# The recurrent unit of an encoder block in another order: both directions gated and scanned first, far halves inverted before the keys, each near half inverted beside the states

## The chip, the cores and the metric

The kernel runs on one core of a Trainium2 chip. The metric is the device time of one execution, in microseconds (us). A core has five engines with an instruction queue each: TensorE (PE) for matrix products and transposes, VectorE (DVE), ScalarE (ACT) and GpSimd (POOL) for elementwise work, and SyncE (SP), which here only issues DMAs. An instruction waits at the head of its engine's queue until what it needs is there, and all behind it wait too.

## The reference

One layer of an encoder for a sequence of 1024 tokens of width 1024. A layer norm, one large projection, dilated window attention with 24 heads, a bidirectional gated recurrence (HGRN2) with 8 heads, a gated merge, and a SwiGLU feed-forward, each with its layer norm:

```python
h = layer_norm(x, ln_in_g, ln_in_b)
proj = h @ w_in[l]                     # 1024 x 11776
aq, ak, av, hq, hf_fwd, hf_bwd, hi, hg, ga, gh = jnp.split(proj, split_idx, axis=-1)
att = dilated_attention(aq, ak, av, slopes)
rec = hgrn2(hq, hf_fwd, hf_bwd, hi, hg, lower_bounds[:, l], hgrn_norm_g[l])
merged = jax.nn.sigmoid(ga) * (att @ w_att_up[l]) + jax.nn.sigmoid(gh) * (rec @ w_hgrn_up[l])
h = layer_norm(DEEPNORM_ALPHA * h + merged @ w_o[l], ln1_g[l], ln1_b[l])
```

The change touches `hgrn2` alone. Per head and direction, with gate f = lb + (1 − lb)·sigmoid(...), key k = 1 − f, query q = silu(...)·128^-0.5 and value v, the chunkwise form is:

```python
q_dec = q * jnp.exp(cum)               # cum: running sum of log f in a chunk
k_inv = k * jnp.exp(-cum)
a = jnp.where(causal_in_chunk, jnp.einsum('bhnik,bhnjk->bhnij', q_dec, k_inv), 0.0)
o_intra = jnp.einsum('bhnij,bhnjv->bhniv', a, v)
u = jnp.einsum('bhnck,bhncv->bhnkv', k * jnp.exp(cum_last - cum), v)
state = d[..., None] * state + uu      # carried from chunk to chunk
o_inter = jnp.einsum('bhnck,bhnkv->bhncv', q_dec, s_start)
```

## The kernel before

**Stages.** The projection (to about 1145 us), the merge with the output projection and a layer norm, and the two halves of the feed-forward. The change lies in the projection stage, `phase1`.

**The stream of products.** `stream` computes the projection by a Strassen-like scheme: a block of 1024 x 512 weights takes 14 products (seven, in the order 1, 2, 6, 5, 7, 3, 4, each for two groups g of columns), and 23 blocks make 322 products. A product is twelve matmuls of 128x128 by 128x512: four slices of k by three terms (L270 to L272), since each operand is split in a high part `hi` and a rest `lo`. ACT makes `w_hi` (L212), POOL `w_lo` (L222), three products ahead. The sums of weights which the scheme needs are made five products ahead: on DVE L652 (`ws`), L653 and L657 (`wa`), on POOL L654. Finished products leave PSUM by `leave`: ACT keeps a copy (`wkeep`, L680), DVE adds the copy to the next product (`plain` L531, `tanhs` L542, `silu2` L556 and L558, with ACT's tanh L557 between them), and a DMA on SP's queue stores the result. Each group has two PSUM banks (tiles `pj`), used in turn.

**The side units.** While the stream runs, one side unit at a time is advanced beside it: `phase1` counts products, and each `yield n` of a unit lets n products pass before its next step. There are eight units `hgrn_side` (one for each recurrent head, in four pairs, a pair after each two heads' columns) and the attention units. Their small products and transposes go to PSUM tiles `sd`.

**One recurrent head.** A chunk has 128 tokens. A direction d has a half of it that is near the place to which the decays are related (`R`, in the buffer `fb`, 8 x 66 columns) and a far half (`A`, one half of the buffer `fa`). `hgrn_dir` does for a direction: ACT makes the gates (L1103 and L1108 into `fa`, L1104 and L1109 into `fb`), POOL sets border columns (L1102, L1107) and makes the keys `t` (L1110); DVE scans `fa` and `fb` to running products (L1115); POOL multiplies the near keys by `R` (L1123). After a yield DVE takes reciprocals of the far half (L1126) and the near half (L1129), in two instructions each of 128 x 256 elements, into the tile `qd`; POOL multiplies the far keys (L1127); DVE multiplies the queries of the far half (L1130) and of the near half (L1131); POOL copies and multiplies three columns `dec` (L1135 to L1137). So the reciprocals of a direction stand right behind its scans, four in a row.

`hgrn_side` goes through direction 0, then 1, loads the output gate `hg` (L734, SP's queue; its buffer is the `fb` of direction 1), transposes the values (L743), and then takes the transposed keys of direction 0 (PE L1145, ACT's copy `hkT` L1146), its states (PE L1161; ACT writes `hS`, L1163, over `fa`; DVE L1169), the keys and states of direction 1, the scores (L1186 to L1190, POOL's sum `ham` L1195), the output (L1212), and the last transposes (L1248) with the gate (DVE L1250, `hg`). ACT's queue issues the store `rec<-hg` (L1251). The buffer of `hg` is the next head's `fb` of direction 1, so that head's L1107 and L1109 wait for this store.

**What sets the order.** The program is written with the Tile framework, whose scheduler places each engine's instructions by simulated readiness and priority. Evictions and weight sums have a priority 1000 steps ahead. `left` notes an eviction by DVE as the latest, and `behind` puts an instruction behind it in the engine's order; it is an order only and no wait. In the kernel before, `behind` is used for the weight sums (L652, L657).

Of the kernel before, what the change touches and what calls it, by code (L numbers as in the profile page):

```python
# [14 lines left out]
OP = mybir.AluOpType  # L15
# [19 lines left out]
CQ = 0.5 * 128 ** -0.5  # L35
# [44 lines left out]
class Block:  # L80
# [152 lines left out]
        self.issued[key] = ins.ins.name  # L233
        return ins

    gone = None

    def left(self, ins):
        self.gone = ins.ins.name

    def behind(self, ins, last=None):

# [848 lines left out]
    def hgrn_dir(self, h, d, st):  # L1091

        nc = self.nc
        ga, gb, gna = (z[:, d, h:h + 1] for z in (self.ga, self.gb, self.gna))
        t3 = st[f"t{d}"].rearrange("p (c i) -> p c i", i=128)
        q3 = st["q"].rearrange("p (c i) -> p c i", i=128)

        A = st["fa"][:, HALF * d:HALF * d + HALF].rearrange("p (c i) -> p c i", i=64)
        B = self.slot(7 + d, "fb", (8, 66))
        if d == 0:  # L1100
            nc.gpsimd.memset(A[:, :, 0:1], 0.0)
            nc.gpsimd.memset(B[:, :, 65:66], 0.0)  # L1102
            nc.scalar.activation(A[:, :, 1:64], t3[:, :, 65:128], AF.Identity, bias=gb, scale=ga)  # L1103
            nc.scalar.activation(B[:, :, 0:65], t3[:, :, 0:65], AF.Identity, bias=gb, scale=ga)  # L1104
        else:
            nc.gpsimd.memset(A[:, :, 63:64], 0.0)
            nc.gpsimd.memset(B[:, :, 0:1], 0.0)  # L1107
            nc.scalar.activation(A[:, :, 0:63], t3[:, :, 0:63], AF.Identity, bias=gb, scale=ga)  # L1108
            nc.scalar.activation(B[:, :, 1:66], t3[:, :, 63:128], AF.Identity, bias=gb, scale=ga)  # L1109
        nc.gpsimd.tensor_scalar(t3, t3, gna, ga, op0=OP.mult, op1=OP.add)  # L1110

        def scan(f, n, rev):
            f = f.rearrange("p c i -> p (c i)")
            f = f[:, ::-1] if rev else f
            nc.vector.tensor_tensor_scan(f, f, self.d1[n], 0.0, op0=OP.mult, op1=OP.add)  # L1115

        scan(A, 64, d == 1)
        scan(B, 66, d == 0)
        far = slice(64, 128) if d == 0 else slice(0, 64)
        near = slice(0, 64) if d == 0 else slice(64, 128)  # L1120
        R = B[:, :, 1:65]
        qd = self.slot(2 + 2 * d, "qd", (8, 128))
        nc.gpsimd.tensor_mul(t3[:, :, near], t3[:, :, near], R)  # L1123
        yield
        for c in (slice(0, 4), slice(4, 8)):
            nc.vector.reciprocal(qd[:, c, far], A[:, c])  # L1126
        nc.gpsimd.tensor_mul(t3[:, :, far], t3[:, :, far], qd[:, :, far])  # L1127
        for c in (slice(0, 4), slice(4, 8)):
            nc.vector.reciprocal(qd[:, c, near], R[:, c])  # L1129
        nc.vector.scalar_tensor_tensor(qd[:, :, far], q3[:, :, far], CQ, A, op0=OP.mult, op1=OP.mult)  # L1130
        nc.vector.scalar_tensor_tensor(qd[:, :, near], q3[:, :, near], CQ, qd[:, :, near], op0=OP.mult, op1=OP.mult)  # L1131
        st["qd", d], st["ki", d] = qd, t3

        dec = st["dec", d] = self.smt.tile([128, 3, 8], F32, name="dec", tag="dec", bufs=4)
        nc.gpsimd.tensor_copy(dec[:, 0, :], A[:, :, 63 if d == 0 else 0])  # L1135
        nc.gpsimd.tensor_copy(dec[:, 1, :], B[:, :, 0 if d == 0 else 65])
        nc.gpsimd.tensor_mul(dec[:, 2, :], dec[:, 0, :], dec[:, 1, :])  # L1137

    def hgrn_keys(self, st, d):

# [9 lines left out]
    def hgrn_states(self, st, d, kT, vT):  # L1150


        nc, dec = self.nc, st["dec", d]
        S = self.slot(6 + d, "hS", (8, 128))
        cs = list(range(8)) if d == 0 else list(range(7, -1, -1))
# [66 lines left out]
    def hgrn_side(self, h, st):  # L1222
        nc = self.nc
        v = self.fetch(5, "hv", self.hg_d[h]["v"])
        st["fa"] = self.slot(6, "fa")
        for d in range(2):
            for _ in self.hgrn_dir(h, d, st):
                yield 1
            if d == 0:
                yield 1  # L1230
        sg = self.fetch(8, "hg", self.hg_d[h]["g"])
        yield 1
        vT = self.turned(v.rearrange("p (k d) -> p k d", k=8), lambda c: v[:, 128 * c:128 * c + 128])
        k0 = self.hgrn_keys(st, 0)
        yield 3
        S = {0: self.hgrn_states(st, 0, k0, vT)}
        k1 = self.hgrn_keys(st, 1)
        yield 3
        S[1] = self.hgrn_states(st, 1, k1, vT)
        yield 3  # L1240
        am = [self.hgrn_scores(st, b) for b in range(2)]
        yield -2
        on = [self.hgrn_out(st, b, am[b], vT, S) for b in range(2)]
        yield 2
        for b in range(2):
            pt = self.ps_sd()
            for jj in range(4):
                nc.tensor.transpose(pt[:, 128 * jj:128 * jj + 128], on[b][:, jj, :], self.ident)  # L1248
            s = slice(HALF * b, HALF * (b + 1))
            nc.vector.scalar_tensor_tensor(sg[:, s], pt, self.ngc, sg[:, s], op0=OP.mult, op1=OP.mult)  # L1250
        nc.scalar.dma_start(self.rec_d[h], sg)  # L1251
# [661 lines left out]
```

## Time and profile before

| | |
|---|---|
| median of three runs | 2074.36 us (2071.59, 2074.36, 2077.41) |
| the profiled execution | 2071.3 us, its span 2069.5 us |
| granted TensorE clock in it | 0.994 |
| PE busy | 2016.2 us, 97% of the span |
| DVE busy | 1325.4 us, 64% |
| POOL busy | 1074.7 us, 52% |
| ACT busy | 953.8 us, 46% |

A row of a group reads: line, engine, operation, output <- inputs, count | busy us, mean ns of one | idle time of the engine just before, and what ended it. A row of a timeline reads: start in us from the beginning of the span, duration, engine, line, operation. A row of a list of waits reads: engine and line of the waiting instruction, what it waited for, and then total us, number of times and the longest. Matmuls are pipelined: each shows about 0.39 us, though they start closer together, so a group of them says less of the time than their starts do. A queue's own waits carry a q behind the engine's name (ACTq, SPq).

### The profile page before, as it was taken

How to read it: one execution, taken by the hardware profiler on the slowest of the kernel's cores; microseconds unless marked ns; L12 is line 12 of the kernel's file. 1: busy time of each engine (PE TensorE's matmuls, PEld its weight loads, DVE VectorE, ACT ScalarE, POOL GpSimd, SP SyncE). 2: the span in 40 equal slices, each digit the busy share in tenths (PEclk: the TensorE clock that was granted, in tenths of full speed). 3: DMA queues.
4: the chain of work that ended last, by engine and by line, in shares of the span. 5: the costliest groups of instructions: out<-in, count | busy, mean ns of one | idle time of the engine just before them, and what ended most of it. 6: DMA issues, size and time to landing. Idle time of an engine off the chain costs nothing. (4 is left out here: it accounts for less than half of the span.)

```text
span 2069.5 us, 30921 instructions
## 1 busy us (share of the span) xinstructions
PE 2016.2 (97%) x10974; PEld 1669.0 (81%) x10974; DVE 1325.4 (64%) x2017; ACT 953.8 (46%) x1968; POOL 1074.7 (52%) x919
## 2 busy tenths in 40 slices
PE   7899999999999999999999999999999999999998
PEld 5688888888887888888888888787888888888876
DVE  6966645884368744776343225547776776758777
ACT  6554455553655436454365432244433333334542
POOL 5766744776356653665536662344665665620012
PEclk9999999999999999999999999999999999999999
DMA  5443433435333452344524376444444443447423
GB/s 157 133 139 125 158 122 105 157 126 173 97 123 133 131 163 93 122 139 137 166 93 154 124 249 219 154 145 139 154 137 138 133 137 132 144 158 270 164 89 127
DMA packets 274844, 297.95 MB, mean 144 GB/s; under 512 B 14017, under 2 KB 207362, under 8 KB 274690
## 3 DMA queue, kind: packets, MB, share of 16 engines
q1 hardware_dynamic: 268384, 274.78, 41.0%
q10 hardware_dynamic: 6306, 21.20, 2.6%
q8 instruction: 86, 1.41, 0.3%
q14 instruction: 68, 0.56, 0.1%
HBM read 201.29 MB, written 94.63 MB: 143 GB/s over the span
## 5 line engine op out<-in xcount | busy, mean ns | idle before, releaser
L222 POOL TENSOR_TENSOR w_lo<-wa,w_hi 128x512 fp32r<-128x512 f32 x272 | 363.2, 1345 | 277.8 <-ACT w_hi L212 250.3
L212 ACT CAST w_hi<-wa 128x512 fp32r<-128x512 f32 x272 | 168.4, 620 | 251.0 <-PE pj L271 165.3
L222 POOL TENSOR_TENSOR w_lo<-wsum,w_hi 128x512 fp32r<-128x512 f32 x88 | 127.7, 1460 | 111.3 <-PE sd L272 60.7
L222 POOL TENSOR_TENSOR w_lo<-f_raw,w_hi 128x512 fp32r<-128x512 f32 x66 | 102.1, 1555 | 55.2 <-ACT w_hi L212 54.0
L208 POOL TENSOR_TENSOR mv<-mv,mhalf 128x1 f32<-128x1 f32 x16 | 10.8, 680 | 208.3 <-DVE mv L207 208.2
L212 ACT CAST w_hi<-wsum 128x512 fp32r<-128x512 f32 x88 | 54.7, 621 | 122.2 <-PE sd L271 118.7
L270 PE MATMUL pj<-xt1hi,w_hi 128*128 128x512 f32 x252 | 99.8, 396 | 3.6 <-DVE evh L531 1.9
L270 PE MATMUL pj<-xb22hi,w_hi 128*128 128x512 f32 x252 | 99.3, 394 | 0.0
L272 PE MATMUL pj<-xb22hi,w_lo 128*128 128x512 f32 x252 | 98.5, 392 | 0.4 <-POOL w_lo L222 0.3
L542 DVE TENSOR_TENSOR evh<-wkeep,pj 128x512 f32<-128x512 f32 x45 | 30.8, 684 | 106.4 <-PE pj L272 61.2
L271 PE MATMUL pj<-xb22lo,w_hi 128*128 128x512 f32 x252 | 98.5, 391 | 0.0
L272 PE MATMUL pj<-xt1hi,w_lo 128*128 128x512 f32 x252 | 98.5, 391 | 0.0
L271 PE MATMUL pj<-xt1lo,w_hi 128*128 128x512 f32 x252 | 98.3, 390 | 0.0
L212 ACT CAST gwsum<-a_raw 128x512 fp32r<-128x512 f32 (+1 forms) x78 | 47.7, 616 | 101.6 <-PE pj L271 47.2
L654 POOL TENSOR_TENSOR wa<-wa,wa 128x512 f32<-128x512 f32 x46 | 65.1, 1424 | 49.5 <-DVE wa L653 44.0
L680 ACT COPY wkeep<-pj 128x512 f32<-128x512 f32 x136 | 79.4, 584 | 21.6 <-DVE evh L558 11.9
L531 DVE TENSOR_TENSOR evh<-wkeep,pj 128x512 f32<-128x512 f32 x66 | 57.5, 879 | 44.5 <-PE pj L272 33.9
L222 POOL TENSOR_TENSOR w_lo<-ws,w_hi 128x512 fp32r<-128x512 f32 x46 | 63.2, 1378 | 43.1 <-ACT w_hi L212 42.9
L222 DVE TENSOR_TENSOR gwkeep<-a_raw,gwsum 128x512 fp32r<-128x512 f32 (+1 forms) x78 | 57.7, 739 | 42.0 <-ACT gwsum L212 39.1
L270 PE MATMUL pj<-xt4hi,w_hi 128*128 128x512 f32 x192 | 76.4, 398 | 3.5 <-DVE evh L531 2.4
L272 PE MATMUL pj<-xt2hi,w_lo 128*128 128x512 f32 x192 | 75.5, 394 | 3.7 <-POOL w_lo L222 3.7
L270 PE MATMUL pj<-xb11hi,w_hi 128*128 128x512 f32 x192 | 76.8, 402 | 1.3 <-DVE wkeep L556 1.3
(421 smaller groups left out, 6585.1 us busy)
## 6 DMA issues: line engine op xcount, KB each, us to landing
wa<-in_w_in_dram SPq DMA_DIRECT2D x184, 256.0 KB, 3.3
f_raw<-in_w_ffn_in_dram SPq DMA_DIRECT2D x44, 512.0 KB, 4.0
a_raw<-gd SPq DMA_DIRECT2D x30, 512.0 KB, 3.6
gd<-fc SPq DMA_DIRECT2D x44, 256.0 KB, 2.0
gd<-fs SPq DMA_DIRECT2D x33, 256.0 KB, 2.1
tg<-evh SPq DMA_DIRECT2D x32, 256.0 KB, 2.3
tg<-tg SPq DMA_DIRECT2D x16, 512.0 KB, 3.6
y<-ahs SPq DMA_DIRECT2D x16, 512.0 KB, 4.6
```

What stands on the lines that cost most here:

```text
L208: nc.gpsimd.tensor_tensor(mv[:, 2:3], mv[:, 2:3], self.mhalf[:, 0:1], OP.pow)
L212: ins = nc.scalar.copy(hi, src) if eng_hi == "act" else nc.vector.tensor_copy(hi, src)
L222: ins = e.tensor_sub(lo, src, hi.bitcast(F32))
L270: nc.tensor.matmul(ps, whi, xhi, start=first, stop=False, **kw)
L271: nc.tensor.matmul(ps, whi, xlo, start=False, stop=False, **kw)
L272: self.product = nc.tensor.matmul(ps, wlo, xhi, start=False, stop=last, **kw).ins.name
L531: self.left(nc.vector.tensor_tensor(o, self.order_src(add, g, kind), s, OP.add))
L542: self.left(nc.vector.tensor_add(t, add, ps))
L654: nc.gpsimd.tensor_sub(a["a21"], a["a22"], a["a11"])
L680: nc.scalar.copy(t, ps)
```

## The change

`hgrn_dir` becomes a sequence of five steps with a yield between them, and `hgrn_side` calls the steps of the two directions in turn:

- Gates, scans, near keys and now also `dec`, of direction 0, then, one product later, of direction 1.
- One product later the reciprocals of the far half and the far keys of direction 0, and one product later those of direction 1.
- One product later the transposed values and the keys of direction 0, and with them the far queries of both directions.
- Two products later the reciprocals and queries of the near half of direction 0; one product later the states of direction 0 and the keys of direction 1; two products later the near half of direction 1 and the load of the output gate; one product later the states of direction 1.

The sum of the yields is as before, so the scores and the output are at the same products. The new function `inverse` makes a half's two reciprocals. Each is put behind an eviction: the second behind the latest one, and the first behind the one before it, which `left` now remembers as `gone2`. The same instructions are issued as before.

```diff
-    gone = None
+    gone = gone2 = None
 
     def left(self, ins):
-        self.gone = ins.ins.name
+        self.gone, self.gone2 = ins.ins.name, self.gone
@@ hgrn_dir
         nc.gpsimd.tensor_mul(t3[:, :, near], t3[:, :, near], R)
-        yield
-        for c in (slice(0, 4), slice(4, 8)):
-            nc.vector.reciprocal(qd[:, c, far], A[:, c])
-        nc.gpsimd.tensor_mul(t3[:, :, far], t3[:, :, far], qd[:, :, far])
-        for c in (slice(0, 4), slice(4, 8)):
-            nc.vector.reciprocal(qd[:, c, near], R[:, c])
-        nc.vector.scalar_tensor_tensor(qd[:, :, far], q3[:, :, far], CQ, A, op0=OP.mult, op1=OP.mult)
-        nc.vector.scalar_tensor_tensor(qd[:, :, near], q3[:, :, near], CQ, qd[:, :, near], op0=OP.mult, op1=OP.mult)
-        st["qd", d], st["ki", d] = qd, t3
-
         dec = st["dec", d] = self.smt.tile([128, 3, 8], F32, name="dec", tag="dec", bufs=4)
...
+        st["qd", d], st["ki", d] = qd, t3
+        yield
+
+        def inverse(o, src):
+            for c in (slice(0, 4), slice(4, 8)):
+                self.behind(nc.vector.reciprocal(o[:, c], src[:, c]), self.gone if c.start else self.gone2)
+
+        inverse(qd[:, :, far], A)
+        nc.gpsimd.tensor_mul(t3[:, :, far], t3[:, :, far], qd[:, :, far])
+        yield
+        nc.vector.scalar_tensor_tensor(qd[:, :, far], q3[:, :, far], CQ, A, op0=OP.mult, op1=OP.mult)
+        yield
+        inverse(qd[:, :, near], R)
+        nc.vector.scalar_tensor_tensor(qd[:, :, near], q3[:, :, near], CQ, qd[:, :, near], op0=OP.mult, op1=OP.mult)
+        yield
@@ hgrn_side
-        for d in range(2):
-            for _ in self.hgrn_dir(h, d, st):
+        steps = [self.hgrn_dir(h, d, st) for d in range(2)]
+        for _ in range(2):
+            for z in steps:
+                next(z)
                 yield 1
-            if d == 0:
-                yield 1
+        vT = self.turned(v.rearrange("p (k d) -> p k d", k=8), lambda c: v[:, 128 * c:128 * c + 128])
+        k0 = self.hgrn_keys(st, 0)
+        for z in steps:
+            next(z)
+        yield 2
+        next(steps[0])
+        yield 1
+        S = {0: self.hgrn_states(st, 0, k0, vT)}
+        k1 = self.hgrn_keys(st, 1)
+        yield 2
+        next(steps[1])
         sg = self.fetch(8, "hg", self.hg_d[h]["g"])
         yield 1
-        vT = self.turned(v.rearrange("p (k d) -> p k d", k=8), lambda c: v[:, 128 * c:128 * c + 128])
-        k0 = self.hgrn_keys(st, 0)
-        yield 3
-        S = {0: self.hgrn_states(st, 0, k0, vT)}
-        k1 = self.hgrn_keys(st, 1)
-        yield 3
         S[1] = self.hgrn_states(st, 1, k1, vT)
```

What this does to the order of the engines is shown for three engines. In these rows a scan prints as SCALAR_TENSOR_TENSOR at L1115, and the line numbers are each kernel's own: the reciprocals L1126 and L1129 are L1133 now, the far keys L1127 are L1136, the far queries L1130 are L1138, the near queries L1131 are L1141, `dec` L1135 to L1137 is L1125 to L1127, the keys L1145 are L1150, the states L1161 are L1166, L1216, L1219 and L1250 of the head before are L1221, L1224 and L1260.

DVE in the second head of the third pair, from its first scan to the evictions L531, before:

```order
L1115 SCALAR_TENSOR_TENSOR fb<-fb,d_859 128x528
L1115 SCALAR_TENSOR_TENSOR fa<-fa,d_856 128x512
L1129 RECIPROCAL qd<-fb 128x4x64 x2
L1115 SCALAR_TENSOR_TENSOR fa<-fa,d_856 128x512
L1126 RECIPROCAL qd<-fa 128x4x64
L1216 TENSOR_REDUCE hss<-hsq 128x4
L1126 RECIPROCAL qd<-fa 128x4x64
L1250 SCALAR_TENSOR_TENSOR hg<-sd,ngc,hg 128x512
L1131 SCALAR_TENSOR_TENSOR qd<-q,qd 128x8x64
L1126 RECIPROCAL qd<-fa 128x4x64 x2
L531 TENSOR_TENSOR evh<-wkeep,pj 128x512 x2
L1219 TENSOR_TENSOR hon<-sd,hss 128x512
```

and now, from the first scan to the third L531:

```order
L1115 SCALAR_TENSOR_TENSOR fb<-fb,d_859 128x528
L1115 SCALAR_TENSOR_TENSOR fa<-fa,d_856 128x512 x2
L1221 TENSOR_REDUCE hss<-hsq 128x4
L1260 SCALAR_TENSOR_TENSOR hg<-sd,ngc,hg 128x512
L1224 TENSOR_TENSOR hon<-sd,hss 128x512
L531 TENSOR_TENSOR evh<-wkeep,pj 128x512 x2
L1133 RECIPROCAL qd<-fa 128x4x64
L1260 SCALAR_TENSOR_TENSOR hg<-sd,ngc,hg 128x512
L531 TENSOR_TENSOR evh<-wkeep,pj 128x512
```

The six reciprocals ahead of the first L531 have gone behind it; only scans and the end of the head before are left there.

What follows there now on DVE, up to the third weight sum:

```order
L1133 RECIPROCAL qd<-fa 128x4x64 x2
L1133 RECIPROCAL qd<-fb 128x4x64
L531 TENSOR_TENSOR evh<-wkeep,pj 128x512
L652 TENSOR_TENSOR ws_6993<-wa_6717,wa_6869 128x512
L652 TENSOR_TENSOR ws_7016<-wa_6778,wa_6904 128x512
L1133 RECIPROCAL qd<-fa 128x4x64
L1133 RECIPROCAL qd<-fb 128x4x64
L1138 SCALAR_TENSOR_TENSOR qd<-q,fa 128x8x64
L1115 SCALAR_TENSOR_TENSOR fb<-fb,d_859 128x528
L653 TENSOR_TENSOR wa_6571<-ws_6993,wa_6571 128x512
```

Reciprocals, the far queries and a scan now stand between the weight sums L652 and L653.

POOL in the last head, from the border columns on, before:

```order
L1107 MEMSET fb 128x8
L222 TENSOR_TENSOR w_lo<-wa_9225,w_hi 128x512
L1110 TENSOR_SCALAR t_9196<-t_9196,gna,ga 128x1024
L1136 COPY dec<-fb 128x8
L1123 TENSOR_TENSOR t_9196<-t_9196,fb 128x8x64
L1127 TENSOR_TENSOR t_9196<-t_9196,qd 128x8x64
L1137 TENSOR_TENSOR dec<-dec 128x8
```

and now:

```order
L1107 MEMSET fb 128x8
L1110 TENSOR_SCALAR t_9196<-t_9196,gna,ga 128x1024
L1126 COPY dec<-fb 128x8
L1123 TENSOR_TENSOR t_9196<-t_9196,fb 128x8x64
L222 TENSOR_TENSOR w_lo<-wa_9016,w_hi 128x512
L1136 TENSOR_TENSOR t_9196<-t_9196,qd 128x8x64
L1127 TENSOR_TENSOR dec<-dec 128x8
```

A weight split `w_lo` stood between the border columns and L1110; now one stands between the near keys L1123 and the far keys L1136.

PE in the last head, around the keys of direction 1, before (`xt4` are the operands of one product, twelve matmuls):

```order
L270 MATMUL pj<-xt4hi,w_hi 128x512
L271 MATMUL pj<-xt4lo,w_hi 128x512
L272 MATMUL pj<-xt4hi,w_lo 128x512
L1145 MATMUL sd<-tabs_sb,t_9196 128x128 x8
L270 MATMUL pj<-xt4hi,w_hi 128x512
```

and now, in the `xt4` product before that one:

```order
L1166 MATMUL sd<-hv,hkT 128x128 x7
L270 MATMUL pj<-xt4hi,w_hi 128x512
L271 MATMUL pj<-xt4lo,w_hi 128x512
L1150 MATMUL sd<-tabs_sb,t_9196 128x128 x8
L272 MATMUL pj<-xt4hi,w_lo 128x512
```

The eight transposes of the keys stood behind the ninth matmul of the second of the two `xt4` products, and stand behind the second matmul of the first, close behind the states of direction 0.

## The prediction

> **What bounds the kernel now.** I read the page's busy shares and clock row first, then the list of PE's waits in the stage that the change touches (the projection, 100 to 1145 us), then the timelines around the longest waits, and last the chain that ended last.
>
> ```profile
> PE 2016.2 (97%) x10974; PEld 1669.0 (81%) x10974; DVE 1325.4 (64%) x2017; ACT 953.8 (46%) x1968; POOL 1074.7 (52%) x919
> ...
> PEclk9999999999999999999999999999999999999999
> ...
> L222 POOL TENSOR_TENSOR w_lo<-wa,w_hi 128x512 fp32r<-128x512 f32 x272 | 363.2, 1345 | 277.8 <-ACT w_hi L212 250.3
> ...
> L654 POOL TENSOR_TENSOR wa<-wa,wa 128x512 f32<-128x512 f32 x46 | 65.1, 1424 | 49.5 <-DVE wa L653 44.0
> ```
>
> PE is busy 97% of the span at the full granted clock, and the next engine, DVE, 64%. So the time is PE's, and the change, which takes no matmul away, can win only where PE stands still.
>
> ```profile
> PE pj L270 <- DVE evh L531: 4.3, 3, 2.4
> PE pj L270 <- ACT wkeep L680: 1.8, 1, 1.8
> PE pj L270 <- DVE wkeep L556: 1.6, 2, 1.3
> PE sd L1212 <- POOL ham L1195: 1.1, 1, 1.1
> PE sd L1161 <- ACT hkT L1146: 1.1, 2, 0.7
> PE sd L1145 <- POOL t L1127: 0.8, 1, 0.8
> ```
>
> These rows (engine and line, what it waited for, total us, times, longest) are all there is to win in that stage but some 0.7 us: 10.7 us together. The longest of them in PE's timeline (start, us, instruction, idle before):
>
> ```profile
> 681.39 0.39 PE L271 MATMUL pj<-xb22lo,w_hi 128*128 128x512 f32 x1
> 681.62 0.39 PE L272 MATMUL pj<-xb22hi,w_lo 128*128 128x512 f32 x1
> 684.39 0.47 PE L270 MATMUL pj<-xt4hi,w_hi 128*128 128x512 f32 x1 [2.38 <-DVE evh L531]
> ```
>
> Matmuls start 0.227 us apart, though each shows 0.39, so a wait costs PE its idle time plus 0.16: here 684.39 − 681.62 − 0.23 = 2.54 for a row of 2.38. A product is twelve matmuls, 2.72 us; its PSUM bank is used again by the fourth product after it, so its eviction may be late by three products, 8.2 us, before PE stands.
>
> What DVE did instead of that eviction, and what it did ahead of L558 at 872.82 (its timeline), with the durations of all reciprocals of L1126 (least, median, most, ns):
>
> ```profile
> 669.83 3.33 DVE L1129 RECIPROCAL qd<-fb 128x256 f32<-128x256 f32 x2
> ...
> 675.00 1.72 DVE L1126 RECIPROCAL qd<-fa 128x256 f32<-128x256 f32 x1
> ...
> 677.19 1.73 DVE L1126 RECIPROCAL qd<-fa 128x256 f32<-128x256 f32 x1
> ...
> 680.01 3.35 DVE L1126 RECIPROCAL qd<-fa 128x256 f32<-128x256 f32 x2
> 683.28 0.96 DVE L531 TENSOR_TENSOR evh<-wkeep,pj 128x512 f32<-128x512 f32 x1
> ```
>
> ```profile
> 864.28 3.35 DVE L1126 RECIPROCAL qd<-fa 128x256 f32<-128x256 f32 x2
> 867.56 2.09 DVE L1115 TENSOR_TENSOR_SCAN fb<-fb,d 128x528 f32<-128x528 f32 x1
> 869.57 3.33 DVE L1129 RECIPROCAL qd<-fb 128x256 f32<-128x256 f32 x2
> 872.82 1.11 DVE L558 SCALAR_TENSOR_TENSOR evh<-evh,wkeep 128x512 f32<-128x512 f32 x1
> ```
>
> ```profile
> L1126 DVE RECIPROCAL qd<-fa x32: 1687/1722/1753, 94.6 to 932.4; 128x256 f32<-128x256 f32 x32
> ```
>
> Six reciprocals (669.83 two, 675.00, 677.19, 680.01 two; 1.65 us from start to start where two follow each other) and the scan between them stand in front of the eviction at 683.28, whose product ended near 681.85 − 3×2.72 = 673.7. At 864 to 873 there are four reciprocals and a scan before L558, which releases the ACT row of the list. The mechanism of the change meets what PE waits for.
>
> **The sum, term by term.** The work is the same: 64 half reciprocals, 32 multiplications, the same transposes and copies; only places move. What lies in PE's path are the waits.
>
> (1) *L531 waits.* In the third pair's second head the new order puts scans only, no reciprocal, before that eviction: 6×1.65 = 9.9 us less work, so it starts at 673.4 or when its product ends (673.7), not at 683.28. The other two waits of this row (1.9 us together) have four reciprocals, 6.6 us, fewer before them. All three go: −(4.3 + 3×0.16) = −4.8. What is late next is the same queue: reciprocals now stand between evictions, one to three at a time (at most 5 us), under the 8.2 us of slack.
>
> (2) *L556 waits*, two, 1.6 us: the same reason, with four reciprocals fewer in front: −(1.6 + 0.3) = −1.9.
>
> (3) *ACT wkeep wait*, 1.8 us. ACT's copy waits for L558 on DVE. The new order has one reciprocal fewer before L556 and none between it and L558; the inverse of the next step stands behind. I take one reciprocal, −1.65; the ends are 0 (something else holds L558 as long) and −1.96 (1.8 + 0.16).
>
> (4) *hkT waits*, two, 1.1 us: PE's state products wait for ACT's copy of the transposed keys. Between the second direction's keys and its states PE had 20 and 23 matmuls at these two places (the first and the last pair's second heads) and has 36 and 34 now; 11 matmuls are 2.5 us, more than either wait. −(1.1 + 0.3) = −1.4; the upper end is 0, since ACT, not the distance, may be late.
>
> (5) *ham and the L1145 row*, 1.9 us, stay: scores are where they were, and the first keys of the third pair's first head stand behind the same matmul as before and still wait for POOL's far product, whose chain begins at a buffer that comes free as late as before. 0.
>
> (6) *A new wait at the last head's second keys.* They move from behind the ninth matmul of one product to behind the second of the product before: 17 matmuls, 3.9 us, less room. Their chain begins at the head before, whose output must be stored before its buffer is overwritten (timelines of PE, DVE, ACT with its queue, POOL, and PE again):
>
> ```profile
> 936.90 0.49 PE L1248 MATMUL sd<-tabs_sb,hon 128*128 128x128 f32 x3
> ```
>
> ```profile
> 938.17 0.74 DVE L1250 SCALAR_TENSOR_TENSOR hg<-sd,ngc,hg 128x512 f32<-128x512 f32 x1
> ```
>
> ```profile
> 938.94 0.33 ACTq L1251 DMA_DIRECT2D rec<-hg  x1
> ...
> 944.06 0.82 ACT L1109 ACTIVATE fb<-t,gb,ga 128x520 f32<-128x520 f32 x1 [2.47 <-DMA rec<-hg]
> ```
>
> ```profile
> 944.15 0.11 POOL L1107 MEMSET fb<- 128x8 f32 x1 [5.71 <-DMA rec<-hg]
> ...
> 945.56 2.14 POOL L1110 TENSOR_SCALAR t<-t,gna,ga 128x1024 f32<-128x1024 f32 x1
> ...
> 947.81 1.19 POOL L1123 TENSOR_TENSOR t<-t,fb 128x512 f32<-128x512 f32 x1
> 948.96 1.29 POOL L1127 TENSOR_TENSOR t<-t,qd 128x512 f32<-128x512 f32 x1
> ```
>
> ```profile
> 944.15 1.05 PE L1161 MATMUL sd<-hv,hkT 128*128 128x128 f32 x8
> 944.96 0.48 PE L270 MATMUL pj<-xt4hi,w_hi 128*128 128x512 f32 x1
> ```
>
> Before: the store (rec<-hg) is issued 0.77 us after the multiply at 938.17, and 5.12 us later (944.06) ACT's gate and POOL's memset of the same buffer start; then L1110 (2.14), L1123 (1.19), the far product (1.29). After: the transposes of 936.90 stand 17 matmuls earlier and the 1.75 us of (1) are gone ahead of them, so they start at 936.90 − 3.86 − 1.75 = 931.3, and the multiply follows at 931.9 (in before it waited for DVE). Store issued 932.7, landed 937.8, gate until 938.6, L1110 until 940.7, L1123 941.9, one weight split now ahead of the far product (1.35, page) 943.3, far product 944.5. PE is at the keys at 944.96 + 2×0.23 − 1.75 = 943.7. Wait 0.8, say +0.9 with the semaphore; ends 0 (another 0.9 us earlier suffices) and +2.5 (two splits in front instead of one).
>
> (7) *Tight weight sums.* A head's reciprocals now also stand among the sums of the next weights (groups of DVE: busy us and mean ns; then the far multiplication's least, median and most):
>
> ```profile
> L652 DVE TENSOR_TENSOR ws<-wa,wa 128x512 f32<-128x512 f32 x40 | 43.1, 1104 | 3.2 <-issue 1.8 <-DMA wa<-in_w_in_dram 1.5
> ...
> L653 DVE TENSOR_TENSOR wa<-ws,wa 128x512 f32<-128x512 f32 x40 | 35.0, 898 | 4.4 <-POOL w_lo L222 4.1
> ...
> L1115 DVE TENSOR_TENSOR_SCAN fa<-fa,d 128x512 f32<-128x512 f32 x15 | 22.0, 1467 | 6.7 <-ACT fa L1103 4.7 <-ACT fa L1108 2.0
> ```
>
> ```profile
> L1130 DVE SCALAR_TENSOR_TENSOR qd<-q,fa x16: 620/682/3168, 112.3 to 954.4; 128x512 f32<-128x512 f32 x16
> ```
>
> In the third pair's second head the worst place is the third product of the next weight block. Behind the eviction of the last product but two of the old block stand three reciprocals, then the next eviction: 0.96 + 3×1.65 + 0.96 − 2.72 = 4.1 us after that second product ended the sums can begin. Then two L652 (2.2), two reciprocals (3.3), the far multiplication (1.1, its mean in the list of groups), a scan (1.4) and two L653 (1.8), two L654 on POOL (2.84) and a split (1.35): 18.1. PE reaches that product's third matmul after six products (16.3), two matmuls (0.45) and four batches of transposes or state products, 0.81 each by 944.15 to 944.96: 20.0. So 1.9 us of room are left, less than two collisions. I allow +1.0; ends 0 and +4.
>
> (8) *Moved at nothing.* The three dec instructions on POOL, of 128x8 elements (a memset of that size took 0.11 at 944.15), go to a head's beginning, where POOL waits for ACT or the store. The gate load (hg) stands later in SP's queue:
>
> ```profile
> SPq L734 <- DVE qd L1129: 48.9, 7, 18.0
> ```
>
> In before this load held the queue 48.9 us in seven waits for the near reciprocal of its buffer, with the weight loads behind it; yet no DMA is in PE's list, so the weights are loaded far enough ahead. Behind the last near inverse it still has some 20 us until the output is gated. If that cover were gone, one weight load (3.3 us) would be late.
>
> Sum: −4.8 − 1.9 − 1.65 − 1.4 + 0.9 + 1.0 = −7.85.
>
> **Does it reach the end?**
>
> ```profile
> 1142.10 0.50 PE pj L272
> ...
> 1219.86 5.50 DMA st_raw<-rec
> ```
>
> The chain that ended last runs through PE from the projection to 1219 us and then over loads and PE again, so time won before 1145 us moves all later. The profiled execution took 2071.3 us, span 2069.5 and 1.8 around it; the sum gives 2063.4 there. The median of the three runs is 2074.36, 3.1 above: 2074.4 − 7.9 = **2066.5**. With every term at its good end: −4.8 − 1.9 − 1.96 − 1.4 = −10.1, 2064.3; with each at its bad one: −6.7 + 0 + 0 + 2.5 + 4 = −0.2, 2074.2.
>
> **A rule against it.** The 32 rows of the far reciprocals lie between 1687 and 1753 ns whatever POOL does, but the far multiplication ranges from 620 to 3168. The Trainium skill ("SBUF — State Buffer", section "Who interferes with whom") says that a DVE instruction with two SBUF inputs and a GpSimd instruction that reads SBUF exclude each other for the whole duration of the one that came first, while one with a single SBUF input does not take part. The trace agrees (steady one-input rows, stretched two-input rows). So moving the multiplications and sums next to each other would cost up to a split, 1.35 us, each. I took means (1.1, 0.9), which hold the collisions of the old order; the other value is rival B's worse case.
>
> **Rivals.**
> A, slower (0.15): in the second heads of the four pairs PE waits for the keys, as in (6), because the chain from the store has no product to spare. For it: 0.8 us at the last head by my own sum. Without (6) the change wins 8.75; to lose 6.2 us it needs (8.75 + 6.2)/4 = 3.7 us a head, a store landing 3 us later than the 5.1 us seen. At 4.5 each: 2074.4 − 8.75 + 18 = 2083.6. Against: the list of waits shows one wait for the far product in eight heads, 0.8 us, and the store would have to take 8 us, not 5.1.
>
> B, sums or weights late. Mild (0.18): 1 us in each second head, 3 more than I allow, and ACT's wait stays (1.65): 2066.5 + 4.65 = 2071.2, within 0.3%. Hard (0.07): four two-input instructions collide, 4×1.35 = 5.4 in 1.9 of room, 3.5 a head, 14 in four: 2066.5 − 1.0 + 14 = 2079.5.
>
> C (0.05): the change doesn't do what it says, because scans (1.47 us each, up to four in a row, 5.9) hold the evictions as the reciprocals did, or the chain after 1219 us doesn't move: 2074.
>
> **How the numbers follow.** Forecast 0.55 at 2066.5, its own range 2063 to 2070 (its ends, less the case that all bad ends come together). About 0.3% (6.2 us) can be told from no change in this kernel; the forecast is faster by 7.9, so close to that bound that 0.04 of its 0.55 falls inside. Faster: 0.55 − 0.04 = 0.51. Same: 0.04 + 0.18 (mild B) + 0.05 (C) = 0.27. Slower: 0.15 (A) + 0.07 (hard B) = 0.22. The range goes from 2060 (best case and 4 us, since the three runs differ by 5.8) to 2081, the light half of A and hard B; it leaves out the heavier half of A and a little on either side, under 0.2.
>
> **What would show it.** Right: the L531 and L556 rows gone from PE's list; reciprocals alternating with evictions on DVE; PE's idle time in 100 to 1145 us near 3 us. Wrong: PE sd rows waiting for POOL's far product (L1136) or ACT's key copies above 3 us (A); rows of L270 or L272 waiting for w_hi or w_lo (B); the same rows as now (C).

## The result, and the profile after

The changed kernel takes 2068.6 us (median of ten runs, 2061.8 to 2071.11) beside 2074.81 us of the kernel before (ten runs on the same chip, 2071.59 to 2077.41): a ratio of 0.9968, 95% interval 0.9957 to 0.9978. Measured once more, beside the last experiments, the ratio was 0.9972 (0.9960 to 0.9983). So the change wins 4.6 to 6.2 us, 0.2 to 0.3%. The profiled execution took 2068.59 us, its span 2066.8, at a granted clock of 0.994 as in the profile before. That is 2.7 us less than the profiled execution before, which was a quick one: it lay 3.5 us under its kernel's median.

The page of the changed kernel, its first line:

```profile
PE 2014.9 (97%) x10974; PEld 1670.4 (81%) x10974; DVE 1324.6 (64%) x2017; ACT 953.3 (46%) x1968; POOL 1078.9 (52%) x919
```

PE is as busy as before, and so are the others. What PE waited for in the projection (100 to 1145 us; total us, times, longest):

```profile
PE sd L1217 <- POOL ham L1200: 3.5, 2, 2.3
PE pj L272 <- POOL w_lo L222: 3.1, 3, 2.1
PE sd L1150 <- POOL t L1136: 1.1, 2, 0.8
PE sd L1150 <- POOL t L1123: 0.5, 1, 0.5
```

All rows of L270, the waits for evictions, are gone, and so is the row for `hkT`: 8.8 us of the old list. What is left is 8.6 us instead of 11.4, because other rows have grown: `ham` from 1.1 to 3.5, the weight split `w_lo` from 0.3 to 3.1, the keys `t` from 0.8 to 1.6.

DVE in the third pair's second head, where six reciprocals stood ahead of an eviction:

```profile
676.58 0.69 DVE L1224 TENSOR_TENSOR hon<-sd,hss 128x512 f32<-128x512 f32 x1 [2.88 <-POOL hss L1223]
677.19 2.03 DVE L531 TENSOR_TENSOR evh<-wkeep,pj 128x512 f32<-128x512 f32 x2
...
681.38 1.03 DVE L531 TENSOR_TENSOR evh<-wkeep,pj 128x512 f32<-128x512 f32 x1
682.33 3.35 DVE L1133 RECIPROCAL qd<-fa 128x256 f32<-128x256 f32 x2
```

The first eviction starts at 677.19, not at 683.28, right behind the end of the head before (`hon`, 676.58), and from there on reciprocals and evictions alternate.

DVE in the second pair's second head, among the weight sums, then POOL and PE there:

```profile
383.46 1.28 DVE L652 TENSOR_TENSOR ws<-wa,wa 128x512 f32<-128x512 f32 x2
384.67 1.74 DVE L1133 RECIPROCAL qd<-fa 128x256 f32<-128x256 f32 x1
386.33 1.69 DVE L1133 RECIPROCAL qd<-fb 128x256 f32<-128x256 f32 x1
387.94 1.22 DVE L653 TENSOR_TENSOR wa<-ws,wa 128x512 f32<-128x512 f32 x2
389.08 1.78 DVE L1138 SCALAR_TENSOR_TENSOR qd<-q,fa 128x512 f32<-128x512 f32 x1
```

```profile
388.64 3.37 POOL L654 TENSOR_TENSOR wa<-wa,wa 128x512 f32<-128x512 f32 x2 [0.90 <-DVE wa L653]
391.97 2.96 POOL L222 TENSOR_TENSOR w_lo<-wa,w_hi 128x512 fp32r<-128x512 f32 x2
```

```profile
387.80 1.09 PE L1150 MATMUL sd<-tabs_sb,t 128*128 128x128 f32 x8 [0.84 <-POOL t L1136]
...
393.73 0.50 PE L272 MATMUL pj<-xt2hi,w_lo 128*128 128x512 f32 x1 [2.07 <-POOL w_lo L222]
```

The two reciprocals at 384.67 and 386.33 stand between the sums L652 and L653; POOL's sums start at 388.64, the split of the product's weights follows at 391.97, and PE stands 2.07 us for it (393.73). Just before, at 387.80, it stands 0.84 us for the far keys. The wait of 2.07 us is the longest of the three in the list's second row.

DVE in the last pair's first head, ahead of the scores (the last fence is the same eviction of the kernel before), and POOL and PE there:

```profile
888.61 1.74 DVE L1133 RECIPROCAL qd<-fb 128x256 f32<-128x256 f32 x1
...
891.35 0.68 DVE L1141 SCALAR_TENSOR_TENSOR qd<-q,qd 128x512 f32<-128x512 f32 x1
...
898.18 0.68 DVE L558 SCALAR_TENSOR_TENSOR evh<-evh,wkeep 128x512 f32<-128x512 f32 x1
...
902.29 0.73 DVE L1196 COPY_PREDICATED amx<-tabs_sb,sd 128x512 f32<-128x512 int32 x1
```

```profile
901.84 2.92 POOL L654 TENSOR_TENSOR wa<-wa,wa 128x512 f32<-128x512 f32 x2 [1.23 <-DVE wa L653]
904.74 1.26 POOL L222 TENSOR_TENSOR w_lo<-wa,w_hi 128x512 fp32r<-128x512 f32 x1
...
906.75 0.72 POOL L1200 TENSOR_TENSOR ham<-amx,amy 64x256 f32<-64x256 f32 x1
```

```profile
907.52 0.49 PE L1217 MATMUL sd<-hv,ham 128*128 128x128 f32 x2 [2.32 <-POOL ham L1200]
```

```profile
895.62 0.68 DVE L558 SCALAR_TENSOR_TENSOR evh<-evh,wkeep 128x512 f32<-128x512 f32 x1
```

A near reciprocal (888.61) and its multiplication (891.35) stand among the states' multiplications. The eviction L558 at 898.18 stood at 895.62 in the trace before; sums, scores' copies (902.29) and POOL's `ham` (906.75, behind two sums and a split) follow it, while PE had come 2.2 us earlier than before (905.20, the start of its wait, for 907.41). It waits 2.3 us.

### The profile page after: what moved, and what is told of

It is laid out like the page before. It is cut to its first block, busy times and chain, and to the rows that moved or that the text cites. A ratio compares the mean times of both kernels' runs of the same rounds, so it can differ in the third digit from the quotient of the medians.

```text
span 2066.8 us, 30932 instructions
## 1 busy us (share of the span) xinstructions
PE 2014.9 (97%) x10974; PEld 1670.4 (81%) x10974; DVE 1324.6 (64%) x2017; ACT 953.3 (46%) x1968; POOL 1078.9 (52%) x919
## 5 line engine op out<-in xcount | busy, mean ns | idle before, releaser
L270 PE MATMUL pj<-xt1hi,w_hi 128*128 128x512 f32 x252 | 99.7, 396 | 0.0
L270 PE MATMUL pj<-xb22hi,w_hi 128*128 128x512 f32 x252 | 99.2, 394 | 0.0
L272 PE MATMUL pj<-xb22hi,w_lo 128*128 128x512 f32 x252 | 98.3, 391 | 0.5 <-POOL w_lo L222 0.3
L272 PE MATMUL pj<-xt1hi,w_lo 128*128 128x512 f32 x252 | 98.6, 391 | 0.0
L680 ACT COPY wkeep<-pj 128x512 f32<-128x512 f32 x136 | 79.1, 582 | 8.3 <-PE pj L272 5.7
L272 PE MATMUL pj<-xt2hi,w_lo 128*128 128x512 f32 x192 | 76.4, 398 | 4.6 <-POOL w_lo L222 4.6
L531 DVE TENSOR_TENSOR evh<-wkeep,pj 128x512 f32<-128x512 f32 x66 | 57.7, 878 | 34.8 <-PE pj L272 24.4
L270 PE MATMUL pj<-xt3hi,w_hi 128*128 128x512 f32 x192 | 77.0, 402 | 0.3 <-ACT wkeep L680 0.3
L270 PE MATMUL pj<-xt2hi,w_hi 128*128 128x512 f32 x192 | 76.4, 401 | 0.7 <-ACT w_hi L212 0.7
```

What stands on the lines that cost most here:

```text
L270: nc.tensor.matmul(ps, whi, xhi, start=first, stop=False, **kw)
L272: self.product = nc.tensor.matmul(ps, wlo, xhi, start=False, stop=last, **kw).ins.name
L531: self.left(nc.vector.tensor_tensor(o, self.order_src(add, g, kind), s, OP.add))
L680: nc.scalar.copy(t, ps)
```

## The experiments

Two questions: which part of the change does it, the sequence of steps or the pins (the reciprocals put behind evictions); and what the new waits cost. Each ratio is to the kernel before, run beside it.

**The steps without the pins**

```diff
-                self.behind(nc.vector.reciprocal(o[:, c], src[:, c]), self.gone if c.start else self.gone2)
+                nc.vector.reciprocal(o[:, c], src[:, c])
```

> The new sequence of steps without the pins: the reciprocals are no longer put behind evictions. Theory P (the pins do the work: the scheduler places instructions by readiness, so it undoes moved steps): as before, 2074.8 within 2 us, with PE's waits for L531 (4.3 us) and L556 (1.6) back. Theory S (the moved steps do the work, scans first and keys further ahead of the states): as after, 2068.6 within 2 us, and no waits for L531.

Ratio 1.0005 (0.9996 to 1.0014). PE's list in the projection begins:

```profile
PE pj L270 <- DVE evh L531: 4.2, 3, 2.4
PE pj L270 <- ACT wkeep L680: 2.5, 1, 2.5
...
PE pj L270 <- DVE wkeep L556: 1.6, 2, 1.3
```

The waits are those of before, since the order of the instructions on all five engines is that of before, one for one: the scheduler places an instruction by its simulated readiness, and the moved steps alone change nothing in what it finds ready first. So theory P holds in this point, theory S doesn't, and this run is at the same time a second measurement of before: the list sums to 13.3 us here and to 11.4 there.

**The pins with the old steps**

```diff
-            nc.vector.reciprocal(qd[:, c, far], A[:, c])
+            self.behind(nc.vector.reciprocal(qd[:, c, far], A[:, c]), self.gone if c.start else self.gone2)
...
-            nc.vector.reciprocal(qd[:, c, near], R[:, c])
+            self.behind(nc.vector.reciprocal(qd[:, c, near], R[:, c]), self.gone if c.start else self.gone2)
```

> The old sequence of steps with the same pins on the reciprocals. Theory P: the three L531 waits (4.9 us of PE) and the L556 wait of the second pair (1.4) go as in after; the third pair's first head keeps six reciprocals ahead of L556, and with three reciprocals between L652 and L653 in the second pair (two in after) the weight-split wait there grows from 2.1 to about 3.8 us; so a part of the gain, 2069 to 2073. Theory S: as before, 2074.8 within 2 us.

Ratio 1.0007 (0.9999 to 1.0016), no gain, which theory P did not foresee. The list:

```profile
PE sd L1161 <- ACT hkT L1146: 3.7, 3, 1.6
PE sd L1145 <- POOL t L1123: 2.1, 1, 2.1
PE sd L1145 <- POOL t L1127: 1.9, 2, 1.2
PE pj L270 <- DVE evh L531: 1.5, 1, 1.5
```

The L531 waits fell from 4.3 to 1.5 us, while P says that they go, and PE now waits 7.7 us for keys (`hkT` and `t`). Neither part wins alone.

**Direction by direction, with pins and late near halves**

```diff
-        for _ in range(2):
-            for z in steps:
+        for z in steps:
+            for _ in range(2):
                 next(z)
                 yield 1
```

> As after, with the pins and the late near halves, but direction 0 is gated, scanned and far-inverted before direction 1 is gated, as in before. Theory K: the old steps with pins alone won nothing because two near reciprocals stood between the far reciprocals on DVE and held up the keys (waits for t and hkT 7.7 us in its list); with the near halves behind the keys it wins as after: ratio to before 0.9955 to 0.9980, keys waits (t and hkT) under 3 us. Rival G: what is needed is that both directions are gated and scanned first; then ratio 0.999 to 1.001 and keys waits above 5 us.

Ratio 0.9962 (0.9948 to 0.9976): theory K. PE's waits for keys are one row:

```profile
PE sd L1217 <- POOL ham L1200: 1.8, 2, 1.2
PE sd L1150 <- POOL t L1123: 1.3, 3, 0.5
```

So gating and scanning both directions first isn't what wins. Beside the run before, this one has the pins too, and the near halves stand behind the first keys. The far queries, `dec` and the transposed values moved along with them, so no run shows the near halves' part alone.

**Only one kind of pin**

```diff
-        def inverse(o, src):
+        def inverse(o, src, pin):
             for c in (slice(0, 4), slice(4, 8)):
-                self.behind(nc.vector.reciprocal(o[:, c], src[:, c]), self.gone if c.start else self.gone2)
+                r = nc.vector.reciprocal(o[:, c], src[:, c])
+                if pin:
+                    self.behind(r, self.gone if c.start else self.gone2)
```

Far halves pinned alone:

> As after, but only the far reciprocals are put behind evictions. The near ones then go back to where DVE is free, between the far reciprocals, and six stand again ahead of an eviction in the third pair's first head. Theory K (near reciprocals between the far ones hold up keys and evictions): the gain is gone, ratio to before 0.9985 to 1.0015. If the place of the far reciprocals is what counts, as after: 0.996 to 0.998.

Near halves pinned alone:

> As after, but only the near reciprocals are put behind evictions. Theory K: at most four far reciprocals stand in a row and the keys are not held up, so most of the gain stays: ratio to before 0.9965 to 0.9985, with an L531 or L556 wait of under 2 us back. If both pins are needed: 0.9985 to 1.0015.

Far alone 0.9982 (0.9973 to 0.9990), near alone 0.9967 (0.9956 to 0.9979). With the near pins alone the time is that of after, as K says, so the pins of the far halves aren't needed. The far pins alone keep more than K says, somewhat over half the gain, just outside the expected range: of the eviction waits only 0.5 us are back in their list, beside 3.4 us for weight splits and 2.1 for `ham`. The list of the near pins has no row for an eviction, though one was expected back; its first two are keys and weight splits:

```profile
PE sd L1152 <- POOL t L1138: 3.3, 2, 2.0
PE pj L272 <- POOL w_lo L222: 2.9, 4, 1.2
```

**No reciprocals at all, in the old order of steps**

```diff
-        for c in (slice(0, 4), slice(4, 8)):
-            nc.vector.reciprocal(qd[:, c, far], A[:, c])
-        nc.gpsimd.tensor_mul(t3[:, :, far], t3[:, :, far], qd[:, :, far])
-        for c in (slice(0, 4), slice(4, 8)):
-            nc.vector.reciprocal(qd[:, c, near], R[:, c])
+        nc.gpsimd.tensor_mul(t3[:, :, far], t3[:, :, far], A)
...
-        nc.vector.scalar_tensor_tensor(qd[:, :, near], q3[:, :, near], CQ, qd[:, :, near], op0=OP.mult, op1=OP.mult)
+        nc.vector.scalar_tensor_tensor(qd[:, :, near], q3[:, :, near], CQ, R, op0=OP.mult, op1=OP.mult)
```

> Before without the 64 half reciprocals: keys and queries are multiplied by the running products themselves, so this part of the computation is left out and the result is another one. It bounds what any place for the reciprocals can win. Theory P: the waits for L531 and L556 and the wkeep wait go, and the hkT waits may, 8.3 to 9.8 us of PE: 2063 to 2066. If the scans or the other side work hold the evictions too, the waits stay above 3 us and the time above 2067.

Ratio 0.9991 (0.9980 to 1.0002), 2071.84 us: the expectation was wrong by 6 us.

```profile
PE pj L272 <- POOL w_lo L222: 3.3, 4, 1.3
PE sd L1141 <- POOL t L1123: 3.0, 3, 1.5
PE sd L1141 <- POOL t L1125: 2.3, 1, 2.3
...
PE pj L270 <- DVE wkeep L556: 0.2, 1, 0.2
```

The eviction waits are gone (the L531 row) or small (L556 0.2), as said; the wait for ACT's copy (L680) falls from 1.8 to 0.9 us. But PE waits 5.3 us for POOL's keys and 3.3 for weight splits; the whole list is 10.5 us. With DVE free the scheduler sets nine of the sixteen batches of transposed keys 10 to 22 matmuls earlier in PE's order, and at two of these places PE waits (0.5 and 1.0 us). The two longest of the waits (1.5 us at 380 and 2.3 at 629) stand where the keys are no earlier than before but 2 to 5 matmuls later; what makes POOL's keys late there isn't shown. So taking 106 us of work off DVE (64 by 1.65) is worth at most 0.2% by itself, and a wait that is taken away is no gain until one knows what PE meets next.

**Where the near halves stand**

```diff
         nc.vector.scalar_tensor_tensor(qd[:, :, far], q3[:, :, far], CQ, A, op0=OP.mult, op1=OP.mult)
-        yield
         inverse(qd[:, :, near], R)
         nc.vector.scalar_tensor_tensor(qd[:, :, near], q3[:, :, near], CQ, qd[:, :, near], op0=OP.mult, op1=OP.mult)
         yield
+        yield
```

> As after, but each near half is inverted with the far queries, as early as the keys, and no longer beside the states. Theory P with my reading that the new ham wait of the last pair's first head (2.3 us) comes from a near reciprocal among the states' multiplications: that wait goes (-2.5), but one reciprocal more stands between L652 and L653 in the second pair's first head and four ahead of L556 in the last pair, about +2: 2066.5 to 2070.5. If putting the near halves beside the states is what wins (rival N): back toward before, above 2072.

Ratio 0.9968 (0.9958 to 0.9979), as after (2065.21 us; the kernel before took 2072.49 beside it): the near halves beside the states win nothing over near halves with the far queries.

```profile
PE sd L1150 <- POOL t L1136: 2.8, 4, 0.9
PE sd L1217 <- POOL ham L1200: 1.6, 2, 1.1
```

The `ham` row falls from 3.5 to 1.6. In the last pair's first head PE comes at the same time as in after (905.09 and 905.20), but DVE's L558 starts at 896.22 and not at 898.18, and the wait is 0.5 us and not 2.3, which bears out its cause. The keys' row L1136 rises from 1.1 to 2.8: an exchange.

**The weight sum noted as an eviction**

```diff
-                    nc.vector.tensor_sub(a["a11"], a["s1"], a["a11"])
+                    self.left(nc.vector.tensor_sub(a["a11"], a["s1"], a["a11"]))
```

> As after, but the weight sum L653 is noted like an eviction, so the reciprocals of the next step go behind it, and the second L652 too. If the late sums cost what PE's list says (w_lo waits 3.1 us in three places, of them 2.1 in the second pair's second head), these waits go and the time falls by 2.5 to 3: 2065.8, within 1.5. If POOL or the SBUF port is what is late there, not DVE's order, the w_lo waits stay and the time is 2068.6.

Ratio 0.9956 (0.9943 to 0.9969), 2063.67 us.

```profile
PE sd L1217 <- POOL ham L1200: 3.6, 2, 2.4
PE pj L272 <- POOL w_lo L222: 1.2, 3, 0.7
```

The `w_lo` row falls from 3.1 to 1.2, the 2.07 us in the second pair are gone, and `ham` stays. So DVE's order was what made the sums late. The ratio's interval overlaps that of after (0.9957 to 0.9978), so the gain itself, some 2.5 us by the middle values, is shown by the waits rather than by the times alone.

**The noted sum with other places of the near halves**

Both near halves one product ahead of the states:

```diff
-        next(steps[0])
+        for z in steps:
+            next(z)
         yield 1
         S = {0: self.hgrn_states(st, 0, k0, vT)}
         k1 = self.hgrn_keys(st, 1)
         yield 2
-        next(steps[1])
```

> The noted weight sum (L653) and both near halves inverted together, one product ahead of the states of direction 0. If the ham wait of the last pair's first head (2.4 us) comes from the near reciprocal that stands among the states' multiplications, it falls under 1 us and the time is 2 us below that of the noted sum alone: ratio to before 0.994 to 0.9955. If the wait only moves to the keys of direction 1 or to the evictions, the ratio stays 0.9955 to 0.997.

The noted sum with the near halves as early as the keys, by the two edits above:

```diff
-                    nc.vector.tensor_sub(a["a11"], a["s1"], a["a11"])
+                    self.left(nc.vector.tensor_sub(a["a11"], a["s1"], a["a11"]))
...
-        yield
         inverse(qd[:, :, near], R)
```

> The noted weight sum (L653) and the near halves inverted with the far queries, as early as the keys. By its parts: the noted sum takes 2.6 us from after, and the early near halves moved after by nothing (ham wait -1.9, keys waits +1.7): ratio to before 0.9945 to 0.9965. A second gain would be seen below 0.9945.

Ratios 0.9942 (0.9924 to 0.9961) and 0.9941 (0.9923 to 0.9959), the second just below the expected range, which by the expectation would be a second gain; its interval covers most of that range, so no second gain is shown.

```profile
PE sd L1217 <- POOL ham L1200: 1.3, 2, 0.7
```

In the first of them `ham` is 1.3 us in two places, none over 0.7, as expected.

**All that won, together, beside the changed kernel once more**

The noted sum, the pair of near halves and the directions one by one, as in the three diffs above:

```diff
+                    self.left(nc.vector.tensor_sub(a["a11"], a["s1"], a["a11"]))
...
+        for z in steps:
+            for _ in range(2):
...
+        for z in steps:
+            next(z)
         yield 1
         S = {0: self.hgrn_states(st, 0, k0, vT)}
```

> Direction by direction as in before, the noted weight sum, and both near halves one product ahead of the states. By the parts measured alone: no ham or weight-split wait above 1.2 us, and the far products of the keys come one product earlier than in the pair of gates: ratio to before 0.992 to 0.995. If the parts win the same waits, it is as with the noted sum and the pair of near halves: 0.994 to 0.996.

The changed kernel itself, with a line of comment ahead (its line numbers are one higher):

> The changed kernel once more, as a reference beside the three others: ratio to before 0.996 to 0.998, and in its profile the same waits as in the first (ham of the last pair's first head above 2 us, the weight split of the second pair's second head near 2).

Combined 0.9932 (0.9919 to 0.9944), 2059.92 us; the changed kernel beside it 0.9972 (0.9960 to 0.9983), 2069.56. The two intervals don't meet: combined is faster than both kernels, but it isn't told apart from the two runs before it. The list of the combined kernel, then that of the changed kernel's second profile:

```profile
PE sd L1150 <- POOL t L1136: 1.2, 1, 1.2
PE pj L272 <- POOL w_lo L222: 1.2, 2, 0.7
...
PE sd L1217 <- POOL ham L1200: 0.7, 1, 0.7
```

```profile
PE sd L1218 <- POOL ham L1201: 4.3, 2, 3.1
PE pj L273 <- POOL w_lo L223: 3.2, 3, 2.1
```

The sums of the whole lists (of one profile each) beside the ratios:

| kernel | waits of PE, 100 to 1145 us | ratio to before |
|---|---|---|
| before, and the steps without pins | 11.4 and 13.3 | 1, 1.0005 |
| pins with the old steps | 11.7 | 1.0007 |
| no reciprocals | 10.5 | 0.9991 |
| far pins alone | 8.7 | 0.9982 |
| after, twice | 8.6 and 10.0 | 0.9968, 0.9972 |
| near pins alone | 9.2 | 0.9967 |
| near halves early | 7.4 | 0.9968 |
| directions one by one | 5.3 | 0.9962 |
| noted sum | 7.2 | 0.9956 |
| noted sum, near pair | 4.4 | 0.9942 |
| noted sum, near early | 5.8 | 0.9941 |
| combined | 5.4 | 0.9932 |

The lists and the times go together, but not us for us: from before to after the mean list falls by 3.05 us and each wait costs 0.16 more than its row (12 waits in before, 9 in after, so 0.5), against 4.6 to 6.2 in the medians. Two profiles of one kernel differ by 1.4 to 1.9 us in the list alone. Where the other 1 to 2.7 us lie isn't settled; the lower end of the intervals, 0.0017 or 3.5 us, doesn't need them. The granted clock explains little of them: its mean was 0.9936 over the twelve later runs of after and 0.9933 over the 29 of before beside them, an estimated 0.6 us. For the combined kernel (14.3 us in the medians, some 7.6 in the lists) it may hold more: its five runs had a mean of 0.9956, and 0.0023 of 2074 us is an estimated 4.8 us if all the time follows the clock. Whether its order brings this clock or only five runs met it isn't shown.

## Why the prediction was right or wrong

The time came 2.1 us above the forecast of 2066.5 and within its range, and the direction was right. The two profiled executions differ by 2.7 us only, where the sum said 7.85, so the terms tell more than the total. PE's idle time was to fall near 3 us and is 8.6: by the lists, with 0.16 a wait, terms (1) to (4) took 10.1 us away, a little more than the 9.75 said, and new waits took 6.8 of them back, where the sum had 1.9. That leaves 3.3 us. That the medians came as near to the forecast as they did is luck in that part.

- **(1), (2): right.** The L531 and L556 rows are gone, and DVE's timeline at 677.19 shows why. The eviction there didn't start with its product's end, as I said, but some 2 us later, since `hon` of the head before stood ahead of it and waited for POOL; the bank's slack covered that.
- **(3): right, a little low.** The whole wait went, not the one reciprocal's 1.65: no reciprocal stands between L556 and L558 now.
- **(4): right.** No row for `hkT` is left.
- **(5): wrong, and the largest miss.** "Scores are where they were" held for PE alone. `ham` went from 1.1 to 3.5 us, because a near reciprocal now stands on DVE among the states' multiplications, so the evictions and sums behind it, and POOL's `ham` behind those sums, came 2.5 us later, while PE, rid of its other waits, came 2.2 earlier. The runs that take the near halves out of that place bring the row to 1.6, 1.3, 1.2 and 0.7. The place alone doesn't make the wait: in the run direction by direction near reciprocals stand there too (880.60 and 883.40), but the states' multiplications begin ahead of them (878.82) and end before the eviction's input is there, and the wait is 0.6 us. The other row of this term, 0.8 us for the far product, didn't stay where it was; it is gone from that place.
- **(6): wrong in its place.** At the last head PE didn't wait:

```profile
933.70 0.75 DVE L1260 SCALAR_TENSOR_TENSOR hg<-sd,ngc,hg 128x512 f32<-128x512 f32 x1 [0.51 <-PE sd L1258]
```

```profile
944.61 1.27 POOL L1136 TENSOR_TENSOR t<-t,qd 128x512 f32<-128x512 f32 x1
```

```profile
944.19 1.72 PE L1166 MATMUL sd<-hv,hkT 128*128 128x128 f32 x14
...
946.21 1.03 PE L1150 MATMUL sd<-tabs_sb,t 128*128 128x128 f32 x8
```

The chain ran as described. From the transposes of `hon` (933.06) to the end of the far product (945.9) it took 12.8 us, where the prediction has 13.2 (931.3 to 944.5). PE took 13.15 us from there to the keys (946.21), where the prediction has 12.4 (to 943.7), and came 0.3 us after them. What it left out are state products: fourteen stand ahead of the `xt4` product now (944.19, the next matmul at 945.67), not the eight of before (944.15 to 944.96), which is 0.7 us more. That all of it came later than said has another reason, PE's wait for `ham` in the head before and the slower clock behind it (last section). A wait for the far product stood instead at the second pair's second head, 0.84 us.
- **(7): right in kind, too small.** 3.1 us in three places instead of 0.3, of them 2.07 at the second pair's second head, against the 1.0 allowed; in the third pair's second head, for which it was worked out, the sums came in time. The run with the noted sum shows that DVE's order was the cause.
- **(8): right.** No DMA row is in PE's list, and the gate load now waits 5.0 us in four places for the near half, not 48.9 in seven.
- **The rivals.** B was nearest: its sign, a row of L272 waiting for `w_lo`, was there, though it didn't turn the time. Its hard case was a collision of two-input instructions with POOL, and these did get longer:

```profile
L1138 DVE SCALAR_TENSOR_TENSOR qd<-q,fa x16: 621/1663/1950, 128.3 to 947.8; 128x512 f32<-128x512 f32 x16
```

The far multiplication's median went from 682 to 1663 ns, as it now runs where POOL is at work (389.08 beside POOL's sums of 388.64, for one), while the reciprocals stayed at 1.7 us. The Trainium skill ("SBUF — State Buffer", section "Who interferes with whom") says that a DVE instruction with two SBUF inputs contends with a GpSimd instruction that reads SBUF, and one with a single SBUF input outside the two-port modes doesn't, and the trace agrees. What reached PE of it is within the 3.1 us of the weight splits, far less than the 14 us of that rival. A's waits for keys came to 1.6 us in all, not 3.7 a head, and C fell with the first list.

That the moved steps do nothing without the pins, and the pins nothing without the late near halves, was not in the prediction, which took the order as one thing.

## What to carry to other kernels

Under a scheduler that places work by readiness, moving a step in the program may change nothing; look at the order of the instructions, and if it must change, tie long low-priority instructions behind the urgent ones of the same engine. Don't take the sum of the waits that a change removes for its gain: each gave the chains behind it time, so follow every engine that came just in time behind it (here POOL's sums, scores and keys) and ask what it does when the bound engine arrives earlier. Weight sums that feed the bound engine are as urgent as evictions: noting one as such took 1.9 us off their row in one line, and 1.4 off the list.

## What was not expected of the hardware

Taking 64 reciprocals of 1.65 us off an engine that is 64% busy changed the time by at most 0.2% (0.9991, 0.9980 to 1.0002). And one profile isn't the kernel: spans of the same instructions in the same order were 2069.5 us (before) and 2065.7 us (the steps without pins), at granted clocks of 0.994 and 0.997, nearly as far apart as the change's 4.6 to 6.2 us, which only the medians of ten and more runs show.

A wait of PE can also cost more than its row. Behind after's `ham` wait of 2.3 us the clock granted from 909 to 912 us is 0.50; over 905 to 915 us it is 0.83, so an estimated 1.7 us of PE's time are lost. That fits with PE being only 1.9 us earlier at the end of the projection in the profile after (1140.17 for 1142.10), where the lists say 3.3. In its second profile the clock is 0.50 from 912 to 915 us, behind a `ham` wait of 3.1, and 0.54 from 394 to 397, behind a weight split's of 2.1. The pins with the old steps (0.50 from 701 to 704, behind 2.1 us) and the kernel without reciprocals (0.50 from 630 to 633, behind 2.3) have one such stretch each. In the fourteen profiles there is no other between 120 and 1140 us. But six more waits of over 2 us were not followed by one: behind the 2.38 us of before the clock is 1.00 from 684 to 694. So what decides it isn't shown, nor what it takes from the runs without a profile.
